# Modulation rows of a two-block network: from VectorE sums to TensorE products in four column strips

## The chip, the cores and the metric

The kernel runs on one core of one Trainium2 chip. The metric is the device time of one execution in microseconds, the median of three runs. One execution was also profiled; its rows are what this document reads.

## The reference, cut to what matters

The network has a first block (attention of three kinds, a gated merge, an FFN) and a second one of two layers (a state-space scan and a differential attention side by side, then an MLP) over two streams of 256 tokens, the latent one and a context. In each layer every norm is followed by a modulation, whose scales, shifts and gates come from one small product of a conditioning vector with a large matrix:

```python
c_act, cc_act = jax.nn.silu(c), jax.nn.silu(c_ctx)        # [1, 1024] and [1024]
for l in range(2):
    mod_l = jnp.split(c_act @ ada_w[l] + ada_b[l], 6, axis=-1)     # ada_w[l]: [1024, 6144]
    mod_c = jnp.split(cc_act @ ada_w[l] + ada_b[l], 6, axis=-1)
    h_l = modulate(xl, norm_mix_g[l], mod_l[0], mod_l[1])          # rmsnorm(x) * g * (1 + scale) + shift
    ...
    xl = xl + mod_l[2] * o_l
    xl = xl + mod_l[5] * sq_relu_mlp(modulate(xl, norm_mlp_g[l], mod_l[3], mod_l[4]), w1[l], w2[l])
```

So for each layer 6144 numbers for each of two vectors are wanted: 25 MB of matrix are read for two rows of results. Everything is float32.

## The kernel before

Activations lie with channels on the 128 partitions, eight tiles of 256 tokens a stream. Dense products are made from exact pairs: a weight piece of 512 KB is loaded into the pool `wr` (seven buffers), ScalarE rounds it to its high part `wh` (L210), VectorE, or at every n-th piece GpSimd, makes the low part `wl` (L213), and TensorE adds three float32r products per tile of 128 channels (`mmT`, L230 to L232; `mmN`, L251 to L253), 24 passes a piece. Some smaller products (scores, scans, transposes, norm sums) are in plain float32.

The order on TensorE is the order in which the code is written (`in_order`): generators of dense products are woven with a list `bg` of side generators, each of which makes one step after each dense one (`weave`, `step`). The other engines' instructions and the loads, nearly all issued by SP, are placed by a planner that goes by priorities and dependences; loads of weights (`wload`) have a priority 100 places ahead of where they stand.

The modulation rows are made on VectorE. `ada_init` (L892) reads both vectors into every partition and makes 2 silu(c) of them as `cb`, [128, 2, 1024]. `ada_step` (L909) loads two tiles of the transposed matrix, [128 rows, 1024 inputs], into buffers of `wr` (L914), and for each tile and stream multiplies by `cb` and sums along the row (L916); a product's sum is one column of `mods`. A layer has 24 such steps, 96 VectorE products. `ada_finish` (L919) adds the bias and makes the gains times 1 + scale.

The steps stand in three places: 12 of the first layer as a side generator of the first block's products (`steps_ada`, L643), one after four steps of the weave; 12 more in the first block's FFN, spread over the first 21 of its 32 channel tiles `up(j)` (L851 to L859); and the second layer's 24 in the first layer's MLP (`adas`, L1655). The FFN's `up` makes a three-tap convolution on VectorE (L828), which frees its PSUM buffer; the MLP's `residual` adds into `xl` and `xc` there (L1728). The PSUM pool `sm` has three buffers, which in the first block the attention heads take in turn.

Of the kernel before, what the change touches and what calls it, by code (L numbers as in the profile page):

```python
# [17 lines left out]
P = 128  # L18
# [6 lines left out]
# columns of the packed per-channel vectors (first block, then each layer of the second)  # L25
# [12 lines left out]
# columns of the row vectors that are read into every partition  # L38
# [14 lines left out]
def const_main():  # L53
    """[128, 6*128 + 512]: identity, triangles, ones, cos, and sin with the sign that rotate-half gives its rows."""
# [14 lines left out]
def const_stick():  # L69
    """[128, 2*384 + 256]: strict-causal 0/1 mask and additive mask of z^T blocks, -(j>=s), -1."""  # L70
    s = np.arange(P)[:, None]
    t = np.arange(P)[None, :]
    strict = (t > s).astype(np.float32)
    m01 = np.concatenate([strict, np.ones((P, P), np.float32), strict], axis=1)
    madd = np.where(m01 > 0, 0.0, NEG).astype(np.float32)
    negu = -(s >= t).astype(np.float32)
    negone = -np.ones((P, P), np.float32)
    return np.concatenate([m01, madd, negu, negone], axis=1)


def const_bias():
    """One-hot of the bucket of each distance [32, 384] and the additive masks [20, 384]; column j holds
    distance 255 - j."""
# [15 lines left out]
class Net:  # L99
# [40 lines left out]
    def constants(self, first):  # L140
        """Loads them; first: only what the first norm needs."""
# [40 lines left out]
    def step(self, bg):  # L182
        """One step of every generator of bg, the oldest first."""
        for g in list(bg):
            if next(g, self) is self:
                bg.remove(g)

    def weave(self, dense, bg):
        """Emit the generator of dense products; after each, one step of the work that hangs on earlier ones."""
# [4 lines left out]
    def wload(self, src, kt=8, eng=None):  # L194
        """src: DRAM view [128, kt * n], a piece of a weight matrix as host_arrays lays it out. Returns a list per k
        of (hi, lo) views [128, n]."""
# [6 lines left out]
        # its turn comes when the last product is through with the piece in its place  # L203
# [12 lines left out]
    def wload2(self, src):  # L216
        """The two pieces, of half the rows each, of 256 columns."""
        return self.wload(src[0], 4) + self.wload(src[1], 4)

    def mmT(self, ps, w, c0, x, t0=None, t1=None, start=True, stop=True, cn=P):  # L220
        """ps [cn, T] += W[:, c0:c0+cn]^T x, x: list per k of (hi, lo) [128, T]."""
# [12 lines left out]
    def mmT2(self, ps, w, x, t0, t1):  # L234
        """mmT of a whole piece; of 512 tokens, in two steps."""
# [6 lines left out]
    def mmN(self, ps, w, c0, cn, x, t0):  # L242
        """ps [128 tokens, cn] = x[:, t0:t0+128]^T W[:, c0:c0+cn]."""
# [23 lines left out]
    def rstd(self, sums, scale, eps):  # L267
        """sums: [128 tokens, n], a column per token tile -> the result likewise, and its diagonal tiles, one per column."""
# [13 lines left out]
    def spread(self, diags):  # L282
        """Diagonal tiles -> their values in every partition, [128, 128 * n] in PSUM."""
# [5 lines left out]
    def norm(self, xs, tmp, out, eng=None, start=False, wait=0):  # L289
        """xs: 8 [128, 256] views over channels. Leaves 1/rms of the tokens, in every partition, in out. A step at  # L290
        a time; eng adds up the squares. start: GpSimd makes them, and nothing else waits for that."""
# [27 lines left out]
    def normed(self, x, g, tmp, h):  # L319
        """h = pairs of rms_norm(x) * g."""  # L320
# [8 lines left out]
    # ---------------------------------------------------------------- first block  # L329
# [11 lines left out]
    def first_block(self, es_x):  # L341
        """Returns the 8 [128, 256] tiles of the residual stream, in a pool of es_x, and the opened scan phase of the
        first layer."""
# [3 lines left out]
        with ExitStack() as es:  # L347
# [11 lines left out]
            # what is free early lies where the next scope's first tiles come  # L359
# [8 lines left out]
            # relative-position bias: vectors over distance, then slid into [query, key] blocks  # L368
# [4 lines left out]
            def bias_tile(pool_, h0, n):  # L373
                """[128 queries, n, 256 keys] of heads h0, h0 + 4, ..."""
# [12 lines left out]
            # x * g: its products become those of the normed x when 1/rms of the token is known  # L387
# [29 lines left out]
            def prodT(src, name, dst, scale=1.0, sl=None):  # L417
                """Two tiles [128 channels, tokens] into dst, a dense block each."""
# [12 lines left out]
            def prodN(src, name, dst, sl=None):  # L431
                """Two tiles [128 tokens, 256 channels] into dst."""
# [25 lines left out]
            def prod_gates(c):  # L458
                """tanh(g/2) = 2 sigmoid(g) - 1"""
# [12 lines left out]
            def prods_c():  # L472
                """From x * g, scaled on the way out."""
# [35 lines left out]
            # attention outputs, channels on partitions: 2 + 4 + 2 tiles of 128  # L509
# [3 lines left out]
            def pv(ops, p0, pt, v, first, last):  # L513
                """ops[p0:p0+64, 256 queries] += V^T P^T; pt [128 keys, 384], v per key block [128, 64]."""
# [9 lines left out]
            def softmax(L1, L0, sink=None):  # L524
                """L1 [128, G, 256], L0 [128, G, 128]: logits -> probabilities, in place."""
# [17 lines left out]
            def transposed(L1g, L0g):  # L543
                """[queries, keys] -> [128 keys, 384]: key block 0 by all queries, key block 1 by the second half."""
# [37 lines left out]
            def heads_b(kv):  # L582
                # query heads j and 4+j share a tile, on the partitions of key heads 0 and 1
# [22 lines left out]
            def heads_c():  # L606
                m01, madd = stick[:, 0:384], stick[:, 384:768]
                negu, neg1 = stick[:, 768:896], stick[:, 896:1024]
                for hd in range(4):
# [6 lines left out]
                    # softplus(z) = max(z, 0) + ln(1 + exp(-|z|))  # L616
# [9 lines left out]
                    # z minus the sum of softplus over the keys from this one to the query  # L626
# [16 lines left out]
            def steps_ada():  # L643
                for i in range(self.NA):
                    for _ in range(4):
                        yield
                    self.ada_step(0, i)
# [43 lines left out]
            def merge():  # L691
                """Gated sum of the branches."""
# [23 lines left out]
            def project():  # L716
                for c in range(4):
                    t = pb.tile([P, 2, 256], F32, tag=f"gate{c}", name=f"hs{c}")
                    if c == 0:
                        # the last tiles of the sum come late  # L720
# [19 lines left out]
            # the context, normalized for the scan phase, in the place of queries, keys and values  # L740
# [30 lines left out]
            with self.in_order():  # L771
# [6 lines left out]
                # what the gates leave  # L778
# [23 lines left out]
        with ExitStack() as es:  # L802
# [45 lines left out]
            na, nj = 24 - self.NA, 21  # L848
            with self.in_order():
                for q in range(4):  # L850
                    mid = self.pairs(pm, 8, 256, "mid")  # L851
                    for jj in range(8):
                        j = q * 8 + jj
                        up(j, mid[jj])
                        if j < nj:
                            for i in range(na * j // nj, na * (j + 1) // nj):
                                self.ada_step(0, self.NA + i)
                        elif j == nj:
# [21 lines left out]
    def add_normed(self, x, hs, g, tmp, shared=()):  # L880
        """x += rms_norm(hs) * g; GpSimd adds the tiles in shared."""
# [9 lines left out]
    # ---------------------------------------------------------------- second block  # L891
    def ada_init(self, pool):  # L892
        """2 silu(c) of both streams in every partition."""
        nc = self.nc
        cb = pool.tile([P, 2, D], F32, tag="cb", name="cb")
        nc.sync.dma_start(cb, self.A["cvec"].rearrange("(o s) d -> o s d", o=1).to_broadcast([P, 2, D]))
        th = pool.tile([P, 512], F32, tag="th", name="th")
        for s in range(2):
            for i in range(2):
                v = cb[:, s, i * 512:(i + 1) * 512]  # L900
                nc.scalar.activation(th, v, AF.Tanh, scale=0.5)
                nc.vector.scalar_tensor_tensor(v, th, 1.0, v, op0=ALU.add, op1=ALU.mult)
        self.cb, self.junk = cb, th.bitcast(mybir.dt.bfloat16)
# [5 lines left out]
    def ada_step(self, l, i):  # L909
        """Modulation rows 256*i .. 256*i+255 of layer l, both streams."""  # L910
        nc = self.nc
        for m in range(2):
# [941 lines left out]
```

## Time and profile before

| | us |
|---|---|
| median of three runs (lowest, highest) | 2663.34 (2662.32, 2667.78) |
| profiled execution, first to last instruction | 2661.6 |
| TensorE busy, 16698 passes | 2551.1 |
| VectorE busy, 3056 instructions | 1936.7 |
| ScalarE busy | 1425.5 |
| GpSimd busy | 872.0 |

The span is what the profile's rows add up to; the median of the timed runs is 1.7 us longer. A busy engine is one with an instruction under way; matmuls are pipelined, so their lengths overlap, and the time from one's start to the next one's is their price. A row that ends in x24 stands for 24 instructions. PE is TensorE, PEld its weight loads, DVE VectorE, ACT ScalarE, POOL GpSimd and SP the engine that issues most loads.

### The profile page before, as it was taken

To read this page: it belongs to the slowest core of one execution; us is meant where nothing else is said; L and a number is where in the kernel's file an instruction comes from. 1 tells how busy PE (TensorE), PEld (TensorE's weight loads), DVE (VectorE), ACT (ScalarE), POOL (GpSimd) and SP (SyncE) were. 2 spreads that over 40 slices of the span, in tenths; PEclk is the share of its full clock that TensorE was granted. 3 is DMA by queue.
4 is the path that set the end of the run, shared out by engine and by line. 5 is a ranking of instruction groups with operands and counts; after the bars stand their busy time and mean duration, and the time that the engine had idled before them with its cause. 6 is when DMAs were issued, how large, how long until landed. Compare 5 with 4: busy or idle time off the path is not lost.

```text
span 2661.6 us, 44600 instructions
## 1 busy us (share of the span) xinstructions
PE 2551.1 (96%) x16698; PEld 2265.6 (85%) x16698; DVE 1936.7 (73%) x3056; ACT 1425.5 (54%) x2722; POOL 872.0 (33%) x749
## 2 busy tenths in 40 slices
PE   7999988999999999999999999899999999999998
PEld 7899988998887888777888978789887888899998
DVE  7887799866666676776646899845777767768754
ACT  5654544554656555666423623235575546655654
POOL 3113533333356565211122311114275542213221
PEclk9999999999999999999999999999999999999999
DMA  7675766764433334332534566534453344356553
GB/s 267 220 228 195 236 204 234 222 190 143 137 119 123 123 127 165 95 98 75 189 127 150 177 223 217 192 103 131 137 163 126 121 157 135 103 161 207 174 186 94
DMA packets 179767, 430.76 MB, mean 162 GB/s; under 512 B 18884, under 2 KB 84610, under 8 KB 179294
## 3 DMA queue, kind: packets, MB, share of 16 engines
q1 hardware_dynamic: 176254, 423.74, 49.1%
q0 software_dynamic: 2720, 3.64, 0.5%
q8 instruction: 132, 2.16, 0.3%
q14 instruction: 85, 0.70, 0.1%
q10 hardware_dynamic: 576, 0.52, 0.1%
HBM read 406.30 MB, written 18.32 MB: 160 GB/s over the span
## 4 chain that ended last, share of the span: by engine, by line
PE 58%; DVE 16%; issue 10%; POOL 7%; DMA 5%; ACT 4%; SPq 0%; POOLq 0%; DVEq 0%; ACTq 0%
PE mm L230 14%; PE mm L231 14%; PE mm L232 14%; DVE th L916 5%; DVE wl L213 4%; PE mm L251 2%; PE mm L252 2%; PE mm L253 2%; DMA Et<-csd 2%; DMA wa<-in_adaT_dram 1%; PE sm L1382 1%; PE lg L1405 1%; POOL E L1172 1%; ACT E L1164 1%; DVE acc L828 1%
## 5 line engine op out<-in xcount | busy, mean ns | idle before, releaser
L210 ACT ACTIVATE wh<-wr 128x1024 fp32r<-128x1024 f32 (+1 forms) x578 | 609.4, 1055 | 660.0 <-PE mm L231 545.9
L230 PE MATMUL mm<-h,wh 128*128 128x256 f32 (+2 forms) x2232 | 768.8, 344 | 11.3 <-ACT r L1628 3.6
L213 DVE TENSOR_TENSOR wl<-wr,wh 128x1024 fp32r<-128x1024 f32 (+1 forms) x466 | 615.9, 1324 | 218.1 <-ACT wh L210 210.1
L231 PE MATMUL mm<-h,wh 128*128 128x256 f32 (+2 forms) x2232 | 743.3, 333 | 2.9 <-DVE h L946 1.5
L232 PE MATMUL mm<-h,wl 128*128 128x256 f32 (+2 forms) x2232 | 743.2, 333 | 0.0
L213 POOL TENSOR_TENSOR wl<-wr,wh 128x1024 fp32r<-128x1024 f32 x112 | 288.4, 2575 | 796.9 <-ACT wh L210 692.5
L230 PEld LDWEIGHTS mm<-h,wh 128*128 128x128 f32 (+1 forms) x2232 | 420.3, 188 | 70.5 <-issue 15.5
L231 PEld LDWEIGHTS mm<-h,wh 128*128 128x128 f32 (+1 forms) x2232 | 420.4, 188 | 51.3 <-issue 5.9
L232 PEld LDWEIGHTS mm<-h,wl 128*128 128x128 f32 (+1 forms) x2232 | 420.1, 188 | 44.1 <-issue 0.4
L916 DVE SCALAR_TENSOR_TENSOR th<-wa,cb 128x1024 bf16<-128x1024 f32 x192 | 267.4, 1392 | 23.3 <-DMA wa<-in_adaT_dram 21.5
L230 PE MATMUL mm<-mid,wh 128*128 128x256 f32 (+1 forms) x832 | 256.6, 308 | 11.8 <-DVE xc L1728 9.6
L231 PE MATMUL mm<-mid,wh 128*128 128x256 f32 (+1 forms) x832 | 255.4, 307 | 1.4 <-DVE mid L257 1.3
L232 PE MATMUL mm<-mid,wl 128*128 128x256 f32 (+1 forms) x832 | 255.2, 307 | 0.5 <-DVE wl L213 0.5
L251 PE MATMUL mm<-wh,h 128*128 128x256 f32 (+1 forms) x704 | 202.7, 288 | 2.2 <-DVE bc L1048 1.2
L230 PE MATMUL mm<-o,wh 128*128 128x256 f32 x592 | 170.8, 288 | 28.4 <-DVE acc L828 17.6
L252 PE MATMUL mm<-wl,h 128*128 128x256 f32 (+1 forms) x704 | 196.9, 280 | 0.0
L253 PE MATMUL mm<-wh,h 128*128 128x256 f32 (+1 forms) x704 | 196.7, 279 | 0.0
L230 PEld LDWEIGHTS mm<-mid,wh 128*128 128x128 f32 x832 | 157.5, 189 | 22.7 <-issue 10.5
L232 PE MATMUL mm<-o,wl 128*128 128x256 f32 x592 | 169.5, 286 | 3.4 <-DVE wl L213 3.3
L231 PE MATMUL mm<-o,wh 128*128 128x256 f32 x592 | 169.2, 286 | 0.0
L231 PEld LDWEIGHTS mm<-mid,wh 128*128 128x128 f32 x832 | 157.4, 189 | 10.3 <-DVE mid L257 2.0
L232 PEld LDWEIGHTS mm<-mid,wl 128*128 128x128 f32 x832 | 157.5, 189 | 9.5 <-DVE wl L213 0.9
(370 smaller groups left out, 4898.7 us busy)
## 6 DMA issues: line engine op xcount, KB each, us to landing
wr<-in_w_in_dram SPq DMA_DIRECT2D x247, 512.0 KB, 3.7
wr<-in_w_mlp_dram SPq DMA_DIRECT2D x144, 512.0 KB, 4.1
wa<-in_adaT_dram SPq DMA_DIRECT2D x96, 512.0 KB, 4.5
wr<-in_w_up_dram SPq DMA_DIRECT2D x64, 512.0 KB, 4.3
wr<-in_w_out_dram SPq DMA_DIRECT2D x32, 512.0 KB, 3.5
wr<-in_w_down_dram SPq DMA_DIRECT2D x32, 512.0 KB, 4.2
wr<-in_w_ssd_o_dram SPq DMA_DIRECT2D x32, 512.0 KB, 3.6
E<-csd SPq DMA_DIRECT2D x24, 512.0 KB, 4.4
```

The costliest lines, as they stand in the source:

```text
L210: nc.scalar.activation(hi, raw, AF.Copy)
L213: eng.tensor_tensor(lo, raw, hi.bitcast(F32), op=ALU.subtract)
L230: nc.tensor.matmul(ps, wh, xh, start=start and k == 0, stop=False)
L231: nc.tensor.matmul(ps, wh, xl, start=False, stop=False)
L232: nc.tensor.matmul(ps, wl, xh, start=False, stop=stop and k == n - 1)
L251: nc.tensor.matmul(ps, xh, wh, start=k == 0, stop=False)
L252: nc.tensor.matmul(ps, xh, wl, start=False, stop=False)
L253: nc.tensor.matmul(ps, xl, wh, start=False, stop=k == n - 1)
L828: nc.vector.scalar_tensor_tensor(a[:, s:], u[:, :256 - s], cw[:, ch * 3 + tap:ch * 3 + tap + 1], a[:, s:], op0=ALU.mult, op1=ALU.add)
L916: nc.vector.scalar_tensor_tensor(self.junk, raw, 0.5, self.cb[:, s, :], op0=ALU.mult, op1=ALU.mult, accum_out=self.mods[l][:, 2 * i + m, s ...
L1164: nc.scalar.activation(v, v, AF.Exp, bias=ncs[:, 2 * sg + c, i:i + 1])
L1172: nc.gpsimd.tensor_tensor(v, v, t, op=ALU.add)
```

## The change

The two vectors are laid with channels on the partitions, and 2 silu(c) stands as the first two of 32 columns per channel tile (`ct`, the others zero). The matrix is read in its own orientation (512 outputs by two tiles of 128 channels are 512 KB). `ada_products` makes 512 outputs at a time: eight plain float32 products, one for each channel tile, with the 32 columns as stationary and 512 matrix columns as moving operand; channel tile k goes to PSUM partitions 32 (k mod 4) and up, so that four column strips of the array each add up two tiles. ScalarE copies the result with the factor 0.5. `ada_rows` then multiplies it by `sel`, whose two columns pick and add up the four strips' rows of each stream, which also turns the results to channels on partitions; VectorE adds the bias. A layer has 12 such groups; they stand in the same three places, 6, 6 and 12. `ada_finish` no longer adds the bias. Comment lines are blank in the new file.

```diff
 def steps_ada():
-    for i in range(self.NA):
-        for _ in range(4):
+    for g in range(6):
+        for _ in range(6):
             yield
-        self.ada_step(0, i)
+        self.ada_products(0, g)
+        for _ in range(2):
+            yield
+        self.ada_rows(0, g)
...
                 up(j, mid[jj])
-                if j < nj:
-                    for i in range(na * j // nj, na * (j + 1) // nj):
-                        self.ada_step(0, self.NA + i)
-                elif j == nj:
+                if j % 5 == 1 and j < 30:
+                    self.ada_products(0, 6 + j // 5)
+                elif j % 5 == 3 and j < 30:
+                    self.ada_rows(0, 6 + j // 5)
+                elif j == 30:
                     self.ada_finish(0, 1)
...
 def ada_init(self, pool):
     nc = self.nc
-    cb = pool.tile([P, 2, D], F32, tag="cb", name="cb")
-    nc.sync.dma_start(cb, self.A["cvec"].rearrange("(o s) d -> o s d", o=1).to_broadcast([P, 2, D]))
-    th = pool.tile([P, 512], F32, tag="th", name="th")
-    for s in range(2):
-        for i in range(2):
-            v = cb[:, s, i * 512:(i + 1) * 512]
-            nc.scalar.activation(th, v, AF.Tanh, scale=0.5)
-            nc.vector.scalar_tensor_tensor(v, th, 1.0, v, op0=ALU.add, op1=ALU.mult)
-    self.cb, self.junk = cb, th.bitcast(mybir.dt.bfloat16)
+    v = pool.tile([P, 2 * KD], F32, tag="cv", name="cv")
+    nc.sync.dma_start(v, self.A["cvecT"])
+    th = pool.tile([P, 2 * KD], F32, tag="cth", name="cth")
+    nc.scalar.activation(th, v, AF.Tanh, scale=0.5)
+    self.ct = pool.tile([P, KD, 32], F32, tag="ct", name="ct")
+    self.sel = pool.tile([P, 2], F32, tag="sel", name="sel")
+    self.rows = pool.tile([P, 512], F32, tag="rows", name="rows")
+    nc.vector.memset(self.ct, 0.0)
+    r = lambda t: t.rearrange("p (k s) -> p k s", s=2)
+    nc.vector.scalar_tensor_tensor(self.ct[:, :, 0:2], r(th), 1.0, r(v), op0=ALU.add, op1=ALU.mult)
+    nc.vector.tensor_reduce(self.sel, self.c("ident").rearrange("p (j r) -> p r j", r=32)[:, 0:2, :], axis=AX.X, op=ALU.add)
...
-def ada_step(self, l, i):
-    nc = self.nc
-    for m in range(2):
-        raw = self.wr.tile([P, D], F32, tag="wr", name="wa")
-        nc.sync.dma_start(raw, self.A["adaT"][l, i][:, m * D:(m + 1) * D])
-        for s in range(2):
-            nc.vector.scalar_tensor_tensor(self.junk, raw, 0.5, self.cb[:, s, :], op0=ALU.mult, op1=ALU.mult,
-                                           accum_out=self.mods[l][:, 2 * i + m, s:s + 1])
+def ada_products(self, l, g):
+    nc = self.nc
+    ps = self.sm_ps()
+    for q in range(4):
+        raw = self.wr.tile([P, 2, 512], F32, tag="wr", name="wa")
+        nc.sync.dma_start(raw, self.A["adaW"][l, g, q].rearrange("p (k n) -> p k n", k=2))
+        for i in range(2):
+            k = 2 * q + i
+            j = 32 * (k % 4)
+            nc.tensor.matmul(ps[j:j + 32, :], self.ct[:, k, :], raw[:, i, :], start=k < 4, stop=k >= 4)
+    nc.scalar.activation(self.rows, ps, AF.Copy, scale=0.5)
+
+def ada_rows(self, l, g):
+    nc = self.nc
+    ps = self.sm_ps([P, 4, 2])
+    for m in range(4):
+        nc.tensor.matmul(ps[:, m, :], self.rows[:, m * P:(m + 1) * P], self.sel, start=True, stop=True)
+    b = self.sm(f"ada_b{l}")[:, 4 * g:4 * g + 4].rearrange("p (m o) -> p m o", o=1).to_broadcast([P, 4, 2])
+    nc.vector.tensor_tensor(self.mods[l][:, 4 * g:4 * g + 4, :], ps, b, op=ALU.add)
 
 def ada_finish(self, l, i):
-    a, b = ((0, 16), (16, 48))[i]
     for s in range(2):
-        nc.vector.tensor_tensor(md[:, a:b, s], md[:, a:b, s], self.sm(f"ada_b{l}")[:, a:b], op=ALU.add)
...
 def adas():
     for _ in range(10):
         yield
-    for i in range(24):
-        self.ada_step(1, i)
-        yield
-        yield
-        if i % 2:
-            yield
+    for g in range(12):
+        self.ada_products(1, g)
+        yield
+        yield
+        self.ada_rows(1, g)
+        yield
+        yield
+        yield
```

## Rows read from the trace of the kernel before

**Rows 1.** the chain of work that ended last: shares of the span by line.

```profile
by line: PE mm L230 14.4%; PE mm L231 14.0%; PE mm L232 13.8%; issue 9.6%; DVE th L916 4.6%; DVE wl L213 3.7%; PE mm L251 2.2%; PE mm L252 2.1%; PE mm L253 2.1%; DMA Et<-csd 1.6%; DMA wa<-in_adaT_dram 1.5%; PE sm L1382 1.3%; PE lg L1405 1.2
```

**Rows 2.** by stretch: length, busy (x) of PE, PEld, DVE, ACT, POOL, clock, DMA.

```profile
40.00:256.00 216.00, 213.77 (x1630) 196.59 (x1630) 177.65 (x316) 124.71 (x233) 51.57 (x27) 1.00 0.67 220
320.00:500.00 180.00, 154.68 (x1253) 151.68 (x1252) 166.08 (x238) 86.06 (x135) 58.30 (x32) 0.97 0.69 225
500.00:600.00 100.00, 99.97 (x866) 99.79 (x865) 70.36 (x102) 62.86 (x91) 31.22 (x22) 1.00 0.67 205
1500.00:1730.00 230.00, 215.68 (x1032) 180.39 (x1031) 217.76 (x346) 86.44 (x128) 37.60 (x18) 0.96 0.63 208
1730.00:1800.00 70.00, 70.00 (x302) 56.70 (x301) 30.15 (x45) 23.39 (x31) 7.22 (x3) 1.00 0.31 102
```

**Rows 3.** the same stretches, L916 alone: length, VectorE busy (x), clock, DMA.

```profile
40.00:256.00 216.00, 63.50 (x96) 1.00 0.67 220
320.00:500.00 180.00, 73.82 (x96) 0.97 0.69 225
1500.00:1730.00 230.00, 131.61 (x192) 0.96 0.63 208
```

**Rows 4.** TensorE's longest wait (total, times, longest), FFN and MLP stretch.

```profile
PE mm L230 <- DVE acc L828: 18.4, 9, 3.8
...
PE mm L230 <- DVE xc L1728: 9.6, 4, 4.7
```

**Rows 5.** groups of TensorE, 1500 to 1730: shapes, count, busy us, mean ns.

```profile
L231 PE MATMUL mm<-h,wh 128*128 128x256 f32 x86 | 24.8, 288 | 0.0
```

**Rows 6.** single lines: duration ns min/median/max, first and last start, shapes.

```profile
L843 ACT ACTIVATE hs<-mm x4: 582/585/586, 403.5 to 463.0; 128x512 f32<-128x512 f32 x4
...
L925 DVE TENSOR_TENSOR mod<-mod,smt x8: 154/178/194, 164.0 to 1729.3; 128x16 f32<-128x16 f32 x4, 128x32 f32<-128x32 f32 x4
...
L569 DVE TENSOR_TENSOR L<-sm,bias x12: 401/416/424, 147.8 to 182.5; 128x256 f32<-128x256 f32 x12
```

**Rows 7.** timeline of TensorE (start us, length): plain fp32 passes.

```profile
781.96 1.88 PE L1249 MATMUL sm<-H,bc 128*128 128x512 f32 x4
783.67 0.49 PE L1196 MATMUL sm<-cst,cv 128*128 128x128 f32 x3
...
685.09 1.93 PE L1032 MATMUL sm<-cst,dtt 128*32 128x128 f32 x16
```

**Rows 8.** timeline: one head's passes, two heads' passes, and their weight loads.

```profile
55.33 0.65 PE L515 MATMUL sm<-pt,sl 128*64 128x256 f32 x2 [1.42 <-ACT pt L635]
55.81 0.38 PE L516 MATMUL sm<-pt,sl 128*64 128x128 f32 x2
56.12 0.38 PE L230 MATMUL mm<-h,wh 128*128 128x256 f32 x1
...
91.29 0.66 PE L515 MATMUL sm<-pt,sl 128*64 128x256 f32 x4
91.77 0.40 PE L516 MATMUL sm<-pt,sl 128*64 128x128 f32 x4
92.10 0.39 PE L230 MATMUL mm<-h,wh 128*128 128x256 f32 x1
...
91.29 0.20 PEld L515 LDWEIGHTS sm<-pt,sl 128*64 128x64 f32 x4
```

**Rows 9.** timeline of TensorE: products of one column.

```profile
267.74 0.50 PE L312 MATMUL sm<-cst,t 128*128 128x1 f32 x4
268.10 0.36 PE L230 MATMUL mm<-h,wh 128*128 128x256 f32 x1
```

**Rows 10.** loads of `wa` (VectorE idle for them; landing us), SP's wait for buffers.

```profile
  DMA wa<-in_adaT_dram: 21.5, 14
...
DMA to landing us min/median/max: 3.1/4.5/8.1
...
SPq L202 <- DVE wl L213: 791.9, 278, 12.9
```

More of the change, by code (lines that the diff above doesn't have):

```diff
@@ L847, in first_block @@
             self.pool_every = self.pv[2]
-            na, nj = 24 - self.NA, 21
             with self.in_order():
@@ L1786, in host_arrays @@
            "lam": np.stack([g[f"lambda_{n}_2"] for n in ("q1", "k1", "q2", "k2")], axis=1).reshape(2, 256),
-           "cvec": np.stack([g["c_2"][0], g["c_ctx_2"]])}
+           "cvecT": np.stack([g["c_2"][0], g["c_ctx_2"]], axis=1).reshape(KD, P, 2).transpose(1, 0, 2).reshape(P, 2 * KD)}
     def cut(w, n):
@@ L1820, in host_arrays @@
     arr["w_dt_2"] = np.concatenate([cut(v[:, 9216:9280], 64) for v in w])
-    arr["adaT"] = np.stack([cut(v, 256).reshape(24, P, KD, 2, P).transpose(0, 4, 3, 2, 1).reshape(24, P, 2 * D)
-                            for v in g["ada_w_2"]])
+    arr["adaW"] = g["ada_w_2"].reshape(2, 4, 2, P, 12, 512).transpose(0, 4, 1, 3, 2, 5).reshape(2, 12, 4, P, D)
     return {n: np.ascontiguousarray(v) for n, v in arr.items()}
-_INS = ["xT", "ctxT", "cvec", "small", "rows", "lam", "cst", "stick", "hot", "bmask", "rel_bias", "w_in", "w_br", "w_out", "w_up",
-        "w_down", "adaT", "w_in_2", "w_dt_2", "w_attn_o_2", "w_ssd_o_2", "w_out_2", "w_mlp1_2", "w_mlp2_2"]
+_INS = ["xT", "ctxT", "cvecT", "small", "rows", "lam", "cst", "stick", "hot", "bmask", "rel_bias", "w_in", "w_br", "w_out", "w_up",
+        "w_down", "adaW", "w_in_2", "w_dt_2", "w_attn_o_2", "w_ssd_o_2", "w_out_2", "w_mlp1_2", "w_mlp2_2"]
 @with_exitstack
```

## The prediction, written before the changed kernel was run

> **What bounds the kernel now.** I read the busy times first (TensorE 2551.1 us of a span of 2661.6), then the chain of waits by line [rows 1]. The six lines of dense products lead it; the work that the change removes, `th` at L916, holds 4.6% (122 us) and its loads 1.5% (40 us). That is an upper mark, not a gain: a chain runs through an instruction even where TensorE has other products to do meanwhile. So I went on to stretches [rows 2]. Without modulation work, 500 to 600 us shows 866 matmul passes in 100.00 us, 115.5 ns each, and 1730 to 1800 us shows 302 in 70.00, 231.8 ns each: TensorE never stops, at 256 and 512 columns. These are the two rates it can hold. Beside them stand the three stretches with modulation work, the first block (40 to 256), its FFN (320 to 500) and the first layer's MLP (1500 to 1730). L916 fills 63.5, 73.8 and 131.6 us of VectorE in them [rows 3], and VectorE is 82%, 92% and 95% busy.
>
> What TensorE loses there follows from counts. FFN: 1253 passes at 115.5 ns are 144.7 us of 180, so 35.3 us are lost. TensorE stands idle 180 - 154.7 = 25.3 of them, 18.4 for the convolution on VectorE [rows 2, 4]; the granted clock averages 0.97, which takes 5.4 us more; the rest is small gaps. MLP: of 1032 passes 257 have 256 columns (three groups like that of [rows 5]), so 775 x 231.8 + 257 x 115.5 ns = 179.6 + 29.7 = 209.3 us of 230; 20.7 are lost, 14.3 of them idle, 9.6 for the sums into `xc` [rows 2, 4]. First block: TensorE is busy 213.8 of 216 us, so it stands 2.2. VectorE is loaded there but hardly holds anybody up. So L916 can give back some 35 + 21 + 2 = 58 us, not its 269.
>
> **What goes.** 192 products with their accumulator reads, 63.5 + 73.8 + 131.6 = 268.9 us of VectorE [rows 3]. In the FFN VectorE then has 166.1 - 73.8 = 92 us of work for 145 us of products, in the MLP 86 for 209, so it stops being late and TensorE is late next, by its own work. Of a full recovery I take off what the undisturbed stretches do not show but a new order may leave: I count 33 of 35 in the FFN, 19 of 21 in the MLP and 2 in the first block, 54 us. Bounds: 40 (the idle time of FFN and MLP alone) to 81 (35 + 21, and 25 in the first block if its many gaps below the waits' resolution were VectorE's too). The set-up goes as well, eight Tanh and eight products of 512 columns and two broadcast loads; they lie beside dense products, and I count nothing. The new set-up (a load of 64 bytes a partition, five small operations, twice) lies at the same place; zero too, and under 4 us if TensorE should wait for it once.
>
> **What comes, on TensorE.** There are 24 groups (6 + 6 + 12). A group has eight products of 512 columns in plain fp32, then four of 2 columns.
>
> Price of a pass: plain fp32 shows two passes for each product, and four passes over 512 columns at L1249 take from 781.96 to 783.67 us, 0.4275 us each [rows 7]. So eight products are 16 passes, 6.84 us one after another. A narrow weight does not help by itself: 16 passes of 128 columns with 32 weight columns, L1032, take 1.93 us, 0.12 each: a quarter of the columns, a little over a quarter of the time [rows 7].
>
> Do strips overlap? No four-strip sequence is in this trace, but one two-strip sequence is. At 55.33 one head's four passes with 64 weight columns keep TensorE until 56.12, 0.79 us. At 91.29 two heads, one writing PSUM partitions 0 to 63 and the other 64 to 127, put eight such passes between 91.29 and 92.10, 0.81 us [rows 8]. Twice the passes in the same time: different column strips run side by side in plain fp32, and in the code all of one head's passes come ahead of the other's, so the second strip did not wait for its turn. Extending this to four strips is an estimate. Each strip then has 2 products of 2 passes, 4 x 0.4275 = 1.71 us a group; with 0.2 for going in and out of the other shape (the 0.79 of [rows 8] less four passes at L1249's rate per column, 0.64, rounded up), 1.9. The other ends are two strips at a time, 3.42 + 0.2, and none, 6.84 + 0.2. I take 1.9, the row with strips being nearer than those without.
>
> The Trainium skill speaks against this: "TensorE: Matmul & The Clock Gate", Part 3, section The mechanism, has weight loads overlap with running matmuls only where the row group differs, and here all eight products use all 128 rows. By it the strips would run one after another, which is the third rival below. The trace disagrees at 91.29: the four weight loads at L515 lie between 91.29 and 91.49, while the first passes run [rows 8]. The same section measures three column strips at 2.38 times one; by that figure eight products would be some 2.9 us, an estimate from the page, and the sum 23 us higher.
>
> The four products of 2 columns are eight passes of a full weight. The nearest row is the 1-column product at L312: four passes between 267.74 and 268.10, 0.09 us each [rows 9]. So 0.8 us. A group costs TensorE 2.7 us, and 24 groups 65 us. All of it lies on the path, since TensorE has no slack once VectorE is no longer late: 16 us in the first block, 16 in the FFN, 32 in the MLP.
>
> **What comes elsewhere.** ScalarE copies 512 columns out of PSUM per group: 0.585 us as `hs` at L843 [rows 6], 14 us in all beside 24% to 58% busy ScalarE [rows 2], two or more dense products ahead of its reader; zero, or 0.6 a group (14) if the reader waits. VectorE adds the bias, 0.18 us as at L925 [rows 6], 4 us. `sm` has three PSUM buffers, shared in the first block with the heads; an additional user there can hold TensorE for one VectorE operation, 0.42 us as L569 has them [rows 6], 12 times in the block: 0 to 5 us, counted zero because VectorE is less loaded than before.
>
> Loads: still 96 of 512 KB in the same weight pool, but by fours, and freed by TensorE at its place in the written order instead of by VectorE whenever it came to it. What is queued behind a late load is now the whole of TensorE's order. Today a load lands 4.5 us after its issue [rows 10], and SP spends 792 us waiting for VectorE's low parts to free weight buffers, that is, loads stand ready long before use [rows 10]. Four of seven buffers are taken; the three left must feed a piece of 24 passes every 2.8 us (FFN) or 5.6 us (MLP), 8.3 us or more for a round of three, against 4.5 for a landing. That cover is enough, so zero; gone, it costs 4.5 us a group. Bytes are the same, the last six of layer 0 spread over more of the FFN (until j = 28, finish at j = 30); nothing reads them before the first layer's residual.
>
> **Sum.** 65 - 54 = +11 us on the span of 2661.6. The median of the timed runs lies 1.7 above it, so 2661.6 + 1.7 + 11 = 2674. Its own range is 2660 to 2690 (gain 42 to 60, cost 58 to 72).
>
> **Rivals.**
> - Faster: VectorE's relief gives more than the waits show. For it: 82% load in the first block [rows 2] and 162 us of chain [rows 1]. Price: gain 81, cost 60, so -21, 2642. Against: TensorE's 2.2 idle us there. It decides where more than some 15 us of the first block's lost time is VectorE's.
> - Two strips at a time: 24 x 1.71 = 41 us more, 2715. For it: only two have been seen. Against: nothing made the second wait.
> - Strips one after another: 24 x 5.13 = 123 more, 2797. The two-strip row speaks against it. That "in four strips" does nothing is this case.
> - TensorE waits for the last load of a group: 24 x 4.5, up to 108 more; with four groups in five late 86, 2760. For it: VectorE waited 14 times for such loads, 21.5 us in all [rows 10]. Against: the buffers' lead.
>
> **How the numbers follow.** Chances: forecast 0.55, faster rival 0.26, two strips 0.09, serial 0.04, late loads 0.06. What a measurement can tell from no change is 0.2%, 5.3 us (2658 to 2668.7). Of the forecast's 0.55, 0.14 lies within that and 0.02 below, 0.39 above; of the faster rival 0.24 below and 0.02 within; the others above, 0.19. So faster 0.26, same 0.16, slower 0.58. The range for 8 in 10 reaches from 2637 (the faster rival with little to spare) to 2718 (two strips), leaving out the two dear rivals and the ends.
>
> **What would show it.** Right: `th` gone; VectorE about 1670 us busy; `rows` copied 24 times; the 512-column passes of the products start some 10 to 30 ns apart in fours, a group done in about 2 us; the waits for `acc` L828 and `xc` L1728 nearly gone; FFN shorter by 15 to 20 us, MLP longer by 10 to 15, first block longer by 12 to 16. Wrong: passes of different strips 0.43 us apart; TensorE waiting for `wa`; a first block no longer than before; dense products in the FFN still slower than 116 ns.

## The result, and the profile after

The changed kernel takes 2684.11 us, median of four runs (2680.08 to 2686.55), against 2665.51 for the kernel before beside it (2662.32 to 2667.78): a ratio of 1.0068, 95% interval 1.0051 to 1.0085. It is slower by 18.6 us; 11 were forecast. The profiled execution has a span of 2684.8, 23.2 longer than the one before.

Busy time of each engine over the span, after:

```profile
PE 2614.0 (97%) x17274; PEld 2296.2 (86%) x17274; DVE 1677.6 (62%) x2686; ACT 1436.4 (54%) x2738; POOL 849.7 (32%) x749
```

TensorE is 63 us busier with 576 more passes (384 of the products, 192 of the turning), VectorE 259 us less busy. In the chain of waits by line, after, `th` has left [rows 1] and the products stand at 2%; no `wa` load is among the lines that it names:

```profile
PE mm L230 18%; PE mm L231 18%; PE mm L232 18%; PE mm L251 2%; PE mm L252 2%; PE mm L253 2%; DMA Et<-csd 2%; PE sm L925 2%; PE sm L1398 1%; DVE wl L213 1%; PE lg L1421 1%; ACT wh L210 1%; ACT E L1180 1%; POOL E L1188 1%; PE sm L1397 1%
```

Stretches after, columns as in [rows 2]: the first block, three windows of the FFN (they overlap), the MLP.

```profile
40.00:266.00 226.00, 224.85 (x1730) 199.53 (x1729) 109.73 (x216) 124.60 (x233) 40.55 (x25) 1.00 0.62 207
320.00:500.00 180.00, 178.46 (x1528) 172.01 (x1527) 118.26 (x184) 107.21 (x168) 62.09 (x45) 1.00 0.71 238
333.00:600.00 267.00, 267.00 (x2282) 257.58 (x2282) 169.08 (x249) 154.08 (x231) 79.56 (x54) 1.00 0.70 232
500.00:600.00 100.00, 100.00 (x853) 96.86 (x852) 63.16 (x89) 54.14 (x79) 27.12 (x19) 1.00 0.67 219
1540.00:1800.00 260.00, 260.00 (x1292) 199.90 (x1291) 94.32 (x155) 84.62 (x114) 24.00 (x10) 1.00 0.53 182
```

Before, 320 to 500 held 1253 passes, 154.7 us busy, at a clock of 0.97 [rows 2]; now TensorE stops for nobody from 333 on, at clock 1.00, and VectorE went from 92% busy to 66% in those 180 us. The MLP shows the same: 260 us without a stop. The waits of TensorE after (total us, times, longest) have neither `acc` nor `xc` among them; these are the four longest of the whole span:

```profile
PE sm L286 <- DVE dg L278: 8.5, 9, 2.4
PE mm L230 <- ACT wh L210: 8.0, 1, 8.0
PE sm L1203 <- POOL xw L1197: 7.2, 6, 2.4
PE sm L312 <- DVE t L303: 3.8, 2, 2.9
```

Single lines after: the products of `wa`, their loads, the copies and the turning. The idle time listed for `wa` names no load of `wa`.

```profile
L925 PE MATMUL sm<-wa,ct x384: 592/592/617, 66.3 to 1781.7; 128*32 128x512 f32 x192
L921 SPq DMA_DIRECT2D wa<-in_adaW_dram x96: 327/328/1087, 30.1 to 1753.8; - x96
its engine sat idle before it (us, times) until:
  issue: 17.7, 57
...
DMA to landing us min/median/max: 3.4/3.8/8.6
```

```profile
L933 PE MATMUL sm<-sel,rows x192: 165/251/272, 76.7 to 1788.6; 128*128 128x2 f32 x192
L926 ACT ACTIVATE rows<-sm x24: 580/598/600, 70.3 to 1782.4; 128x512 f32<-128x512 f32 x24
```

One group in the MLP, timeline of TensorE after (start us, length, xcount of passes in a row):

```profile
1585.30 0.39 PE L231 MATMUL mm<-mid,wh 128*128 128x512 f32 x1
1585.53 0.40 PE L232 MATMUL mm<-mid,wl 128*128 128x512 f32 x1
1585.85 1.93 PE L925 MATMUL sm<-wa,ct 128*32 128x512 f32 x16
1587.71 0.50 PE L230 MATMUL mm<-mid,wh 128*128 128x512 f32 x1
1588.05 0.39 PE L231 MATMUL mm<-mid,wh 128*128 128x512 f32 x1
...
1593.08 0.40 PE L232 MATMUL mm<-mid,wl 128*128 128x512 f32 x1
1593.32 0.95 PE L933 MATMUL sm<-sel,rows 128*128 128x2 f32 x8
1594.13 0.49 PE L230 MATMUL mm<-mid,wh 128*128 128x512 f32 x1
1594.45 0.40 PE L231 MATMUL mm<-mid,wh 128*128 128x512 f32 x1
```

Sixteen passes of 512 columns hold TensorE from 1585.85 to 1587.71, 1.86 us (1.85 in all 24 groups): the four strips run side by side. Inside, four passes, one for each strip, make a set; their starts lie 6 to 7 ns apart, and the next set follows 409 to 434 ns after the last start. The first eight weight loads, those of two sets, are done by 1586.01, while the first set runs and before the second starts at 1586.31:

```profile
1585.85 0.16 PEld L925 LDWEIGHTS sm<-wa,ct 128*32 128x32 f32 x8 [0.36 <-issue]
```

Dense passes beside the group start 0.23 us apart, but from the one ahead of it to its own start it is 0.32 us, from the first behind it to the next 0.34, and from the first behind the turning to the next 0.32.

**Where the time went.** Windows of equal times don't hold equal work, so I cut the traces at the same dense pass: all kernels here have 14424 passes of L230 to L232 and L251 to L253, and a stretch is the time from the start of its first pass to the start of the next stretch's first (the last one ends where the last dense pass starts). To know what the modulation costs on either engine, one kernel below keeps only its loads ("loads only").

| passes, us | 0–1500 first block | 1500–1800 | 1800–3900 FFN | 3900–8100 | 8100–9300 MLP | 9300–end |
|---|---|---|---|---|---|---|
| before | 247.2 | 49.2 | 281.8 | 931.0 | 275.9 | 857.7 |
| after | 262.3 | 48.8 | 266.2 | 934.9 | 293.3 | 860.1 |
| loads only | 246.4 | 49.2 | 246.7 | 932.6 | 257.1 | 861.9 |

After less before: +15.1 first block, -15.6 FFN, +17.4 MLP; that is 16.9 of the 22.8 between the two sums. The other 6 lie in three stretches with next to no modulation work. "Loads only" has some 6 more than before there too, so TensorE's new products don't make them, and the traces of the other kernels differ there by as much (931.0 to 938.1 us in the fourth stretch, 852 to 863 in the last). I take them for chance; the medians hold hardly any of them (18.6 against 16.9).

### The profile page after: what moved, and what is told of

It reads as the page before. It is cut to its first block, busy times and chain, and to the rows that moved or that the text cites. A ratio compares the mean times of both kernels' runs of the same rounds, so it can differ in the third digit from the quotient of the medians.

```text
span 2684.8 us, 45353 instructions
## 1 busy us (share of the span) xinstructions
PE 2614.0 (97%) x17274; PEld 2296.2 (86%) x17274; DVE 1677.6 (62%) x2686; ACT 1436.4 (54%) x2738; POOL 849.7 (32%) x749
## 4 chain that ended last, share of the span: by engine, by line
PE 73%; issue 7%; POOL 6%; DVE 5%; ACT 4%; DMA 3%; SPq 0%; POOLq 0%; DVEq 0%; ACTq 0%
PE mm L230 18%; PE mm L231 18%; PE mm L232 18%; PE mm L251 2%; PE mm L252 2%; PE mm L253 2%; DMA Et<-csd 2%; PE sm L925 2%; PE sm L1398 1%; DVE wl L213 1%; PE lg L1421 1%; ACT wh L210 1%; ACT E L1180 1%; POOL E L1188 1%; PE sm L1397 1%
## 5 line engine op out<-in xcount | busy, mean ns | idle before, releaser
L213 DVE TENSOR_TENSOR wl<-wr,wh 128x1024 fp32r<-128x1024 f32 (+1 forms) x466 | 604.9, 1299 | 330.9 <-ACT wh L210 306.5
L230 PE MATMUL mm<-h,wh 128*128 128x256 f32 (+2 forms) x2232 | 772.4, 346 | 10.0 <-ACT r L1644 3.5
L232 PE MATMUL mm<-h,wl 128*128 128x256 f32 (+2 forms) x2232 | 745.5, 334 | 0.0
L213 POOL TENSOR_TENSOR wl<-wr,wh 128x1024 fp32r<-128x1024 f32 x112 | 274.0, 2446 | 878.8 <-ACT wh L210 801.3
L230 PEld LDWEIGHTS mm<-h,wh 128*128 128x128 f32 (+1 forms) x2232 | 422.4, 189 | 73.8 <-issue 15.1
L232 PEld LDWEIGHTS mm<-h,wl 128*128 128x128 f32 (+1 forms) x2232 | 421.9, 189 | 43.8 <-issue 0.6
L230 PE MATMUL mm<-mid,wh 128*128 128x256 f32 (+1 forms) x832 | 255.7, 307 | 0.3 <-ACT mid L256 0.3
L232 PE MATMUL mm<-mid,wl 128*128 128x256 f32 (+1 forms) x832 | 253.3, 304 | 0.0
L251 PE MATMUL mm<-wh,h 128*128 128x256 f32 (+1 forms) x704 | 204.1, 290 | 2.5 <-DVE xl L1746 1.5
L253 PE MATMUL mm<-wh,h 128*128 128x256 f32 (+1 forms) x704 | 198.1, 281 | 0.0
L230 PE MATMUL mm<-o,wh 128*128 128x256 f32 x592 | 168.7, 285 | 8.0 <-ACT wh L210 8.0
L230 PEld LDWEIGHTS mm<-mid,wh 128*128 128x128 f32 x832 | 156.3, 188 | 15.6 <-PE sm L925 3.4
L232 PE MATMUL mm<-o,wl 128*128 128x256 f32 x592 | 167.5, 283 | 1.3 <-DVE wl L213 1.3
L232 PEld LDWEIGHTS mm<-mid,wl 128*128 128x128 f32 x832 | 156.2, 188 | 7.9
L251 PEld LDWEIGHTS mm<-wh,h 128*128 128x128 f32 x704 | 134.5, 191 | 6.3 <-issue 4.0
```

The costliest lines, as they stand in the source:

```text
L213: eng.tensor_tensor(lo, raw, hi.bitcast(F32), op=ALU.subtract)
L230: nc.tensor.matmul(ps, wh, xh, start=start and k == 0, stop=False)
L232: nc.tensor.matmul(ps, wl, xh, start=False, stop=stop and k == n - 1)
L251: nc.tensor.matmul(ps, xh, wh, start=k == 0, stop=False)
L253: nc.tensor.matmul(ps, xl, wh, start=False, stop=k == n - 1)
```

## The experiments

Times are medians, ratios to the kernel before on the same chip with 95% intervals. Line numbers of kernels that keep both ways are some higher than in the kernel after.

**1. Passes of 16 columns instead of 512.** What in a group depends on the columns?

```diff
-nc.tensor.matmul(ps[j:j + 32, :], self.ct[:, k, :], raw[:, i, :], start=k < 4, stop=k >= 4)
-nc.scalar.activation(self.rows, ps, AF.Copy, scale=0.5)
+nc.tensor.matmul(ps[j:j + 32, 0:16], self.ct[:, k, :], raw[:, i, 0:16], start=k < 4, stop=k >= 4)
+nc.scalar.activation(self.rows[:, 0:16], ps[:, 0:16], AF.Copy, scale=0.5)
...
```

> The changed kernel with its products cut from 512 matrix columns to 16, so that most modulation rows stay at the bias; the loads, the order, the copies and the turning products stay. Theory (TensorE pays for its columns): a group falls from 1.95 us to between 0.4 and 0.9 us, so 24 groups give 25 to 37 us back and the kernel stands at 2647 to 2659. Rival (the price is fixed: change of shape, the loads held by fours, PSUM buffers): under 10 us back, 2674 or more.

2642.5 us, ratio 0.9903 (0.9871 to 0.9935): 41.6 less than after, 1.73 a group; that is more than the 25 to 37 expected. The timeline of TensorE in it:

```profile
64.59 0.32 PE L926 MATMUL sm<-wa,ct 128*32 128x16 f32 x16
64.84 0.70 PE L520 MATMUL sm<-sl,qb 64*128 64x256 f32 x2
```

Sixteen passes now take 0.25 us instead of 1.85. The columns' time lies wholly on the path, and a price per pass or per weight load beyond these 0.25 us is out: the gain is a little more than the 1.60 of the passes themselves. (ScalarE's copy is shorter here too; TensorE does not wait for it in either kernel.) What a group still costs fits the parts that do not hang on columns: 2642.5 is 29.2 us above number 11, which has no products, so 1.2 us a group. The passes (0.25), the turning (0.81) and the slower dense passes around them, which stay as they were after, 0.30 a group in FFN and MLP, make 1.36.

**2. One strip.** All eight channel tiles in the first column strip, one sum; the copy and the turning (not shown) take 32 rows.

```diff
-                j = 32 * (k % 4)
-                nc.tensor.matmul(ps[j:j + 32, :], self.ct[:, k, :], raw[:, i, :], start=k < 4, stop=k >= 4)
+                j = 0
+                nc.tensor.matmul(ps[j:j + 32, :], self.ct[:, k, :], raw[:, i, :], start=k == 0, stop=k == 7)
...
```

> The changed kernel with all eight channel tiles in one strip of 32 columns, and the turning product reading that strip alone. Theory (strips run side by side and TensorE has no slack): 16 passes one after another, 6.84 us a group instead of 1.85, so 24 x 5.0 = 120 us more, 2795 to 2815. Rival (TensorE has slack in these stretches that takes the products in): under 60 us more, below 2745.

2818.32 us, ratio 1.0562 (1.0526 to 1.0598): 134 above after (2795 to 2815 were expected).

```profile
67.77 7.05 PE L925 MATMUL sm<-wa,ct 128*32 128x512 f32 x16
74.75 0.70 PE L520 MATMUL sm<-sl,qb 64*128 64x256 f32 x2
```

6.98 us for the same sixteen passes, 5.13 more than with strips, and 24 x 5.13 = 123. Most of the other 11 lie in the same stretches (MLP 358.2 against 293.3, 65 for 12 groups, 62 by the passes); what they are was not followed. So four strips are worth 3.8 times in the passes.

**3. TensorE only in the FFN.** First block and MLP as before, on VectorE; six groups in the FFN, where [rows 2, 4] showed VectorE late. The cut of the edit is against the kernel before.

```diff
-                                self.ada_step(0, self.NA + i)
...
+                        if j % 5 == 1 and j < 30:
+                            self.ada_products(0, 6 + j // 5)
+                        elif j % 5 == 3 and j < 30:
+                            self.ada_rows(0, 6 + j // 5)
```

> Only the six groups in the first block's FFN go to TensorE; the first block's 12 steps and the MLP's 24 stay on VectorE as before. Theory (what VectorE's lateness costs is given back where it was late, and each stretch stands for itself): the FFN's own share of the change, 16.5 us of price against 31 given back, so 2665 - 15 = 2650 (2645 to 2656). Rival (the stretches hang together, the gain in the FFN comes from the first block's order or is lost behind it): 2658 or more.

2650.74 us, ratio 0.993 (0.991 to 0.9951): faster than both kernels, and inside the 2645 to 2656 of its theory. FFN 267.6 us, first block 246.8, as the two kernels have them; the MLP is 268.2 with the code of before, 7.7 shorter there than in the trace of before.

```profile
333.00:600.00 267.00, 267.00 (x2273) 259.15 (x2272) 167.79 (x246) 153.49 (x231) 79.97 (x55) 1.00 0.67 225
1500.00:1730.00 230.00, 222.84 (x1040) 185.34 (x1041) 214.90 (x338) 81.88 (x118) 33.60 (x13) 0.98 0.64 208
```

FFN: no stop. The MLP moves though its code does not. Here are its stretch in the kernel before, its stretch in this kernel, and 3 us of the kernel before just behind one of its stops; then, from the kernel before again, the passes around that stop:

```profile
1517.00:1792.90 275.90, 265.15 (x1203) 218.09 (x1202) 230.74 (x359) 94.71 (x131) 35.64 (x13) 0.98 0.57 187
1506.80:1775.00 268.20, 261.04 (x1202) 215.46 (x1201) 229.77 (x357) 94.54 (x131) 37.58 (x13) 0.99 0.59 191
1676.00:1679.00 3.00, 3.00 (x8) 2.32 (x8) 3.00 (x6) 0.00 (x0) 0.00 (x0) 0.50 0.31 109
```

```profile
1675.65 0.76 PE L230 MATMUL mm<-mid,wh 128*128 128x512 f32 x1 [4.69 <-DVE xc L1728]
...
1676.64 0.63 PE L232 MATMUL mm<-mid,wl 128*128 128x512 f32 x1
1677.07 0.63 PE L230 MATMUL mm<-mid,wh 128*128 128x512 f32 x1
```

Before, TensorE stands idle 10.7 us of the stretch, here 7.2. Behind the stop of 4.7 us the granted clock is 0.50, the lower of its two levels (1.2 GHz), and passes of 512 columns start 0.43 us apart instead of 0.23. So a stop can cost more than its own length. Seven traces have this MLP's code unchanged (before, this one and numbers 4, 5, 6, 9 and 10); there it takes 268.2 to 277.5 us. TensorE's idle time in it runs from 7.2 to 12.9 us, and the time lost to the clock (the stretch's length times what its mean granted clock lacks of 1.00) from 1.7 to 6.8. Loads only (number 11), with no stop there and a clock of 1.00, takes 257.1; that and the two losses add up to each of the seven times within 2.2 us. Each time comes from a single trace, and the one of this kernel was its fastest run.

**4. Half of the FFN on each.** Three groups on TensorE and six steps on VectorE, one at every fifth channel tile.

```diff
+                        if j in (1, 11, 21):
+                            self.ada_products(0, 9 + j // 10)
...
+                        if j % 5 == 0 and j < 30:
+                            self.ada_step(0, self.NA + j // 5)
```

> In the FFN three groups go to TensorE and six steps stay on VectorE, one at every fifth channel tile up to the 26th; elsewhere all as before. Theory (VectorE is late only when nearly full; with half its modulation work gone it is at about 85% and keeps up): price 8.3 us against 25 to 31 given back, 2665 - 20 = 2645 (2640 to 2650). Rival (every VectorE product delays somebody in proportion): half of 31 given back, 15.5 - 8.3 = 7 us, 2658.

2658.45 us, ratio 0.9962 (0.9946 to 0.9978): the rival's number. TensorE's longest wait there, in 320 to 600:

```profile
PE mm L231 <- DVE acc L830: 7.4, 6, 2.0
```

Six waits, and there are six steps. The FFN takes 271.4 us, 24.7 above number 11; less 3 x 3.25 us for its three groups (19.5 us for six, below) some 15 of the 35 us lost before are left. So half the work on VectorE leaves a little under half the loss, and the theory that VectorE need only fall below full falls.

**5 to 7. Is it how VectorE's work stands?** If a step of four products (6.15 us) in front of a convolution is the harm, smaller or more thinly spread steps should cost less. All three keep everything on VectorE: half steps over the same 21 tiles; whole steps over 30 tiles; half steps over 30 tiles and in the MLP too. The cut of the edit, of the first, is against the kernel before; the second only has 30 for 21.

```diff
+    def ada_half(self, l, i, m):      # one load and the two products of its tile
...
-            na, nj = 24 - self.NA, 21
+            na, nj = 48 - 2 * self.NA, 21
```

> The kernel before, with the FFN's 12 VectorE steps cut into 24 halves (one load, two products of 1.3 us) over the same 21 channel tiles; nothing on TensorE. Same VectorE load, smaller bunches ahead of the convolution that frees a PSUM buffer. Theory A (bunches: TensorE waits for what stands behind a step's four products): the FFN's lost 41 us fall by a third to a half, 2665 - 14 to -20 = 2645 to 2651. Theory B (load: VectorE at over 90% is late however it is cut): 2660 to 2668.

> The kernel before, with the FFN's 12 whole steps spread over 30 channel tiles instead of 21: the same bunches, VectorE's load in that stretch 10 points lower. Theory A (bunches): each step still holds TensorE, 2660 to 2668. Theory B (load): the lost time falls by half or more, 2640 to 2650.

> VectorE alone, halves everywhere but in the first block: the FFN's 24 over 30 channel tiles, the MLP's 48 with one step of the weave between them and a second after every fourth (60 in all, as before). Both theories: the FFN's gain, A 15 to 25 of it from the cutting, B 15 to 25 from the spreading; in the MLP (22 us lost, load as before) A gives back another 7 to 11, B nothing. A: 2630 to 2645; B: 2642 to 2652.

2665.32 us, ratio 0.9989 (0.9972 to 1.0006); 2663.91, 0.9979 (0.9966 to 0.9992); 2659.91, 0.9969 (0.9957 to 0.9981). The first lies where theory B had it, the second where theory A had it, the third above both. FFN 280.9, 281.4 and 279.8 us against 281.8: next to nothing. The third gains 8.6 us by the medians, 5.1 of its trace in the MLP (270.8), which also moves where nothing is changed (number 3). The wait for `acc` in the first (320 to 500), and in the second (320 to 570) with its stretch:

```profile
PE mm L230 <- DVE acc L828: 22.7, 11, 3.6
```

```profile
PE mm L230 <- DVE acc L828: 20.5, 13, 3.6
320.00:570.00 250.00, 229.15 (x1868) 226.47 (x1867) 214.60 (x307) 128.59 (x198) 82.81 (x47) 0.96 0.66 219
```

Before it was 18.4 us in 9 waits [rows 4]: now there are more waits, of the same length in the first (2.1 us in the mean, 2.0 before) and shorter in the second (1.6), and not less in sum. In the second VectorE is busy 86% instead of 92% and as much is lost. Neither theory held: here the loss follows the amount of VectorE's work in the FFN, not its grain, nor its place within it.

**8. Half steps in the MLP, TensorE in the FFN.** Number 3 with the MLP's 24 steps in halves; the edit is against number 3.

```diff
-                for i in range(24):
-                    self.ada_step(1, i)
+                for i in range(48):
+                    self.ada_half(1, i // 2, i % 2)
...
```

> The FFN's six groups on TensorE as in the run with the FFN alone (2650.7), the first block's steps on VectorE, the MLP's on VectorE in halves. A: 2650.7 - 7 to -11 = 2640 to 2644. B: 2649 to 2652.

2648.78 us, ratio 0.992 (0.9901 to 0.9939); MLP 268.0 us against 268.2 in number 3. Halves do nothing there either, as theory B had it, and the two kernels can't be told apart.

**9 and 10. More of the work in the first block.** There VectorE's steps seemed free [rows 2]: 16 or 18 steps instead of 12, and four or three groups in the FFN instead of six. The edit is against number 3.

```diff
-        self.NA = 12
+        self.NA = 16                                      # the second: 18
...
-                    for _ in range(4):
+                    for _ in range(3):                    # the second: 3, 3, 2
```

> As the run with the FFN alone on TensorE (2650.7), with 16 steps instead of 12 on VectorE in the first block (three yields between them instead of four) and four groups instead of six on TensorE in the FFN. Theory (VectorE's modulation work costs almost nothing where nobody waits behind it, 1 us per 67 in the first block): 2 x 2.75 = 5.5 us less, 2645 (2641 to 2649). Rival (VectorE at 93% of that stretch is late there as it was in the FFN, some 0.4 us per us of work): 22 us of work cost 9, 2654.

> The same with 18 steps in the first block and three groups in the FFN: VectorE nearly full there (178 + 34 of 216 us). Theory: 3 x 2.75 = 8.3 us less than 2650.7, less 0 to 5 for what now comes late, 2642 to 2647. Rival (0.4 us per us of work): 33 us cost 13, 2656.

2652.8 us, ratio 0.9945 (0.9926 to 0.9965), and 2655.24, 0.9951 (0.9933 to 0.9969). Against number 3 (2650.74) neither gains; the rivals had 2654 and 2656. The FFN gave 5.8 and 9.2 us, the first block took 7 and 13. First block, 20 to 260 us, in number 3 and in the second of these:

```profile
20.00:260.00 240.00, 235.16 (x1784) 216.62 (x1783) 197.88 (x358) 135.77 (x253) 57.55 (x31) 0.99 0.67 222
```

```profile
20.00:260.00 240.00, 230.44 (x1697) 211.49 (x1697) 212.62 (x384) 130.66 (x245) 47.33 (x27) 0.96 0.71 241
```

With 7% more VectorE work TensorE makes 87 passes fewer in the same 240 us, and the granted clock falls to 0.96 beside it. The free room in the first block ends between 12 and 16 steps.

**11. Loads only.** The products, the copy and the turning are left out, so the modulation rows are their bias; the 96 loads stay.

```diff
-                nc.tensor.matmul(ps[j:j + 32, :], self.ct[:, k, :], raw[:, i, :], start=k < 4, stop=k >= 4)
-        nc.scalar.activation(self.rows, ps, AF.Copy, scale=0.5)
...
-        for m in range(4):
-            nc.tensor.matmul(ps[:, m, :], self.rows[:, m * P:(m + 1) * P], self.sel, start=True, stop=True)
...
-        nc.vector.tensor_tensor(self.mods[l][:, 4 * g:4 * g + 4, :], ps, b, op=ALU.add)
+        nc.vector.tensor_copy(self.mods[l][:, 4 * g:4 * g + 4, :], b)
```

> The changed kernel without its TensorE work: products, copies and turning products are left out, the modulation rows are the bias alone; the 96 loads stay. Theory (24 groups cost 2.75 us each and nothing else does): 2684 - 66 = 2618 (2612 to 2624). Rival (part of the 19 us over the kernel before lies in loads or order, not in TensorE's work): 2630 or more.

2613.33 us, ratio 0.9796 (0.9774 to 0.9818). It is 54.7 us below the kernel before (2668.05 beside it) and 70.8 below after, inside the 2612 to 2624 of its theory. FFN and MLP in it:

```profile
325.00:570.00 245.00, 245.00 (x2120) 245.00 (x2118) 161.22 (x236) 150.08 (x222) 75.93 (x54) 1.00 0.72 240
1500.00:1750.00 250.00, 250.00 (x1118) 206.08 (x1117) 104.31 (x155) 88.23 (x116) 26.57 (x11) 1.00 0.56 184
```

The FFN's passes are 115.6 ns apart, the undisturbed rate of [rows 2], with all loads still moving: the loads cost nothing there. No product holds their buffers in this kernel; that buffers held by fours cost nothing is read from the trace after, where TensorE waits for no load.

## Why the prediction was right in direction, and which term was small

**What VectorE gives back: 54 forecast, 54.7 measured.** From the table, before less loads only: 0.8 in the first block (2 forecast), 35.1 in the FFN (33), 18.8 in the MLP (19). Counting passes against the undisturbed rate of the same trace found what the share of the chain (122 us) and VectorE's 269 busy us did not. The faster rival, which wanted 25 us from the first block, falls with the 0.8. The medians agree: 2668.05 - 2613.33 = 54.7. So close a match is partly luck. The median before moved between 2665.5 and 2668.5 from one set of its runs to the next, the MLP's 18.8 is one trace's (11 to 20 in the seven traces of number 3), and of the 20.7 us that the forecast counted as lost in the MLP's window, 3.6 are a wait for ScalarE's `r` that the change leaves as it was. Before and after:

```profile
PE mm L230 <- ACT r L1628: 3.6, 1, 3.6
PE mm L230 <- ACT r L1644: 3.5, 1, 3.5
```

**What TensorE pays: 65 forecast, 71.6 measured.** After less loads only: 15.9, 19.5 and 36.2 us, 24 groups at 2.98 instead of 2.7. This is the term that was mis-sized. Its parts: 1.85 for the sixteen passes (1.71 forecast), 0.81 for the turning (0.8). What was too small is the 0.2 for "going in and out of the other shape": it measured 0.30, on top of sixteen passes that take 0.14 us more than forecast. In the FFN and MLP the dense pass ahead of the products holds TensorE 0.09 us longer than others of its shape, the first behind them 0.11 to 0.12, the first behind the turning 0.09 to 0.10: 0.30 a group (means over 18 groups, against a quick pass, the 15th percentile, of the same line and shape before; the timeline shows one group). So 1.85 + 0.81 + 0.30 = 2.96. I had read the price of the change off the end of a head's passes [rows 8], which leaves out what the dense passes ahead and behind take longer. In the first block a group costs 2.65, and the forecast of 16 holds. Why it is less there is not shown: ahead of four of its six groups and behind two the dense passes are longer there too. The traces differ by some 3 us in that block with the same code (245.2 to 248.4 in seven), which is 0.5 a group and more than the 0.8 that VectorE gives back there.

**By stretch.** First block +15.1 (12 to 16 forecast), FFN -15.6 (15 to 20 shorter), MLP +17.4 (10 to 15 longer, so missed: twelve groups at 3.02 instead of 2.7 are 3.8 us more).

**Strips.** The row with two strips carried over to four: 6.98 us in one strip, 1.85 in four. Both rivals on strips are out. The Trainium skill, "TensorE: Matmul & The Clock Gate", Part 3, section The mechanism, lets weight loads overlap running matmuls only where the row group differs; all these products use all 128 rows, and eight of their weight loads are done while the first set of passes runs, so the trace disagrees. That sentence is on weight loads; the next section, Measured speedup vs the span model, has three column strips at 2.38 times one, so the page does not say that strips run one after another, as the prediction took it. The 2.9 us for eight products that the prediction worked out from 2.38 are 1.85 here: four strips give 3.8 in the passes.

**Late loads.** TensorE waited for no load of `wa`, median landing 3.8 us; the buffers' lead held, as costed at nothing. ScalarE's copy, VectorE's bias and the PSUM buffers at zero hold as well: nothing of them is among TensorE's waits in FFN or MLP, and the first block shows the group's own price and no more.

**What the experiments add.** The exchange rate of VectorE's work differs by stretch. Modulation work on VectorE against time lost, that is, the stretch less the same one in loads only (number 11):

| | VectorE us | lost us | |
|---|---|---|---|
| first block, 12 / 16 / 18 steps | 63.5 / 85.4 / 98.6 | 0.8 / 7.3 / 13.6 | free, then 0.3 to 0.5 per us |
| FFN, 6 / 12 steps | 36.2 / 73.8 | 15 / 35.1 | 0.4 to 0.5 per us |
| MLP, 24 steps | 131.6 | 18.8 (11 to 20 in seven traces) | 0.1 to 0.2 per us |

(FFN with 6 steps: 271.4 - 246.7, less 3 x 3.25 for its groups.) Two steps, a group's worth, cost 5.9 us in the FFN on VectorE and 3.25 on TensorE; 0.1 against 2.65 in the first block; 0.9 to 1.7 against 3.0 in the MLP. So the change pays in the FFN alone, which is number 3: 2650.74. Open stays why the FFN loses nearly half a microsecond for each one of VectorE's, whatever its grain, and why TensorE stops more or less often in the MLP with the same code there. Placing VectorE's steps in the later stretches was not tried.

## What to carry to other kernels

Price an engine's relief by stretch: passes counted against the rate of an undisturbed stretch of the same trace gave it here within a few microseconds, the engine's busy time and its share of the chain did not. Work that moves to the engine which is the bound costs its full time plus what its neighbours lose at the change from one kind of product to the other, 0.1 us at three places a group here, so move it only where the stretch pays for it. A kernel with the work left out and its loads kept splits a small net change into its two large terms. One trace of a stretch is not enough where the engine stops: the same code took 268 to 277 us.

## What the runs showed of the hardware

Four column strips of TensorE in plain fp32, each with all 128 rows, run side by side: starts 6 to 7 ns apart, 1.85 us for sixteen passes of 512 columns against 6.98 in one strip, and weight loads of the next set go on beside running passes of the same rows (1585.85 to 1586.01). With 16 columns the sixteen passes and their weight loads take 0.25 us. Between dense float32r passes, going to plain fp32 products of 32 weight columns costs 0.09 us and coming back 0.11 to 0.12, whether they have 512 columns or 16; going to plain fp32 with full weights costs nothing that is seen (1593.08 to 1593.32 is 0.24), and coming back from it 0.09 to 0.10. After a stop of 4.7 us the granted clock was 0.50 and passes started 0.43 us apart instead of 0.23.
